# A two-layer RWKV-7 / convolution backbone: the block merge of each triangular inverse split from its solve, with buffers of its own time

## The chip, the cores and the metric

The kernel runs on one core of a Trainium2 chip. The metric is the device time of one execution in microseconds (us); shorter is better. The engines are called PE (TensorE, matrix products), DVE (VectorE), ACT (ScalarE), POOL (GpSimd) and SP (SyncE, which issues transfers).

## The reference, cut to what matters

Layer 0 mixes tokens by a bidirectional RWKV-7 recurrence over 16 heads of 64 channels, next to a gated short convolution. A context of 256 tokens runs first and hands its final states to the latent sequence of 512 tokens. Layer 1 is a Conformer convolution module. The change lies in layer 0's recurrence:

```python
def wkv_scan(S0, r, decay, k, v, kk, a, reverse):
    def step(S, inp):
        r_t, w_t, k_t, v_t, kk_t, a_t = inp
        sa = jnp.einsum("bhvk,bhk->bhv", S, -kk_t)
        S = (S * w_t[:, :, None, :]
             + sa[..., None] * (kk_t * a_t)[:, :, None, :]
             + v_t[..., None] * k_t[:, :, None, :])
        return S, jnp.einsum("bhvk,bhk->bhv", S, r_t)
    ...
yac, S_f, S_b = rwkv_seq(rwkv_prep(hc, ...), zero, zero, r_k, lnx_w, lnx_b, ctx_out)
ya, _, _ = rwkv_seq(rwkv_prep(h, ...), S_f, S_b, r_k, lnx_w, lnx_b, True)
yb = bg * dwconv(cg * xb, sc_w, seg_len)
y = jnp.concatenate([ya * jax.nn.silu(za), yb * jax.nn.silu(zb)], axis=-1) @ w_out
```

## The kernel before, in words

**Tiling.** The recurrence is computed in chunks of 64 tokens. Inside a chunk it is a triangular system, whose 64x64 inverse is formed for each head, direction and chunk; from chunk to chunk only a state is handed on. The work is cut into 12 "states": four of the context (c0 to c3, four heads and four chunks each) and eight of the latent sequence (l0 to l7, two heads and eight chunks each). Both directions and all heads of a state lie side by side, so that 32 inverses are formed at once.

**One state passes through these steps.**
- *Preparation*: projections of r, k, v (`prep_ctx`, `prep_lat`), then `light`, which runs `lightz` for each direction: decays and gates into the tiles P, a and kd (each of these tags has one buffer), and from them the factors AR and BK.
- *heavy*: the products `pal` on PE, masked by DVE into E (L601), the transposed BK (`pbl`, copied by ACT at L612), the diagonal 32x32 blocks of E copied by ACT into the tile Nt (L618), v transposed (`pvl`, L629) and the bonus (`pbonl`, L636).
- *solve*: DVE transposes Nt into X (L650) and inverts all 32x32 diagonal blocks by 31 elimination steps of two operations each (L656, L658); the result is Y.
- *merge* (inside `solve`, L659 to L681): two inverted 32x32 blocks become the inverse of a 64x64 block. DVE transposes Y into R1 (L661) and R1 into R2 (L662), ACT copies R1 into E (L667), PE multiplies 64 blocks (called M1 below), ACT copies the product to Gs (L676), PE multiplies 64 blocks again (M2), and ACT copies that into E (L681). R1 is the tile Nt, R2 is Y's tile and Gs a half of X's tile.
- *chain*: over the chunks in turn, PE's products into `zo` and `uh`, ACT's copies of them to O (Ol, L756) and UV (L762), and DVE's update of the state H (L769). A chain step reads E, and its products are pinned to the written order.

There is one Nt for all states, and E, UV and BKt of the latent states exist twice.

**Order.** The main loop runs chain(s) and then, by the letters of `STAGE`, the work of the states after it: P prepares s+2, L and H are `light` and `heavy` of s+2, S is `solve` of s+1, O the bonus of s+1, F the fills and the output of s, C the gated convolution. A scheduler takes the letters' order as priorities and merges these streams into one order for each engine, so PE fills the chain's waits with wide products: `pcg`, `pxb`, `pbg` and `pzb` of the convolution branch, and in the context `plr`, `plk` and others. Each wide product runs three times, since weights are split into a high and a low half (`wh`, `wl`, L126 on ACT and L127 on DVE). All matrix products go through the helper on L57.

Of the kernel before, what the change touches and what calls it, by code (L numbers as in the profile page):

```python
# [15 lines left out]
P = 128  # L16
# [15 lines left out]
CONV_AFTER = (0, 2, 7, 6)  # L32
PA_ORDER = ((0, 1), (1, 0), (1, 1), (0, 0))
HEAVY = ("VBOAN", "ANBV")
STAGE = ("OFPLSH", "OSPLHFC")
FILL_R = (0, 0, 2, 3, 4, 4, 4, 4)
FILL_Z = (0, 1, 1, 1, 3, 3, 3, 3)
ZR = (slice(0, 64), slice(64, 128))
# [13 lines left out]
def kernel(ctx: ExitStack, tc: tile.TileContext, I: dict, out: bass.AP):  # L52
# [3 lines left out]
    def mm(o, lhsT, rhs, start, stop):  # L56
        return T.matmul(o, lhsT, rhs, start=start, stop=stop)  # L57
# [36 lines left out]
    def col(nm, j, n=1):  # L94
        gi, off, _ = colpos[nm]
        return colt[gi][:, off + j : off + j + n]
# [80 lines left out]
    def w(tag, name, dt=F32):  # L177
        return wk.tile([P, SIZE.get(tag, 512)], dt, tag=tag, name=name, bufs=NBUF.get(tag, 1))

    def ch3(t, x=CH):  # L180
        return t.rearrange("p (c x) -> p c x", x=x)

    def small(name, shape):
        return cvp.tile(shape, F32, tag=name, name=name)
# [11 lines left out]
    Nt = small("Nt", [P, 16, 32])  # L196
# [196 lines left out]
    def prep_ctx(b, between=None):  # L393
        st = state(False, b)
        for which in (1, 2):
            st["rkv"[which]] = t = w("rkv"[which] + "_", "rkv"[which] + st["nm"])
            for p, cs in st["parts"]:
                project(p, which, t[:, cs])
                if between:
                    between()  # L400
        return st
# [240 lines left out]
    def solve(st):  # L642
        nm, E = st["nm"], st["E"]
        Xt = w("X", "X" + nm)
        X = Xt.rearrange("p (a b) -> p a b", b=32)
        Yt = w("Y", "Y" + nm)
        Y = Yt.rearrange("p (a b) -> p a b", b=16)
        tmp = w("xtmp", "xtmp" + nm)
        nc.gpsimd.dma_start(Y, I["unit"])
        V.transpose(X.rearrange("p (r s) t -> p t r s", r=2),  # L650
                    Nt.rearrange("p q t -> p t q").unsqueeze(2).to_broadcast([P, 32, 2, 16]))
        for i in range(31, 0, -1):
            c0 = i // 2
            m = 16 - c0
            tv = tmp[:, : i * m].rearrange("p (a b) -> p a b", b=m)
            V.tensor_tensor(out=tv, in0=X[:, :i, i : i + 1].to_broadcast([P, i, m]),  # L656
                            in1=Y[:, i : i + 1, c0:].to_broadcast([P, i, m]), op=ALU.mult)
            V.tensor_tensor(out=Y[:, :i, c0:], in0=Y[:, :i, c0:], in1=tv, op=ALU.add)  # L658
        R1 = Nt  # L659
        R2 = Yt.rearrange("p (a b) -> p a b", b=32)  # L660
        V.transpose(R1.rearrange("p q (c r) -> p c r q", r=2), Y.rearrange("p (a b) c -> p c a b", a=2))  # L661
        V.transpose(R2, R1)  # L662
        Gs = Xt[:, 0:512].rearrange("p (a b) -> p a b", b=32)
        for z in range(2):
            for b in range(2):
                rs = slice(64 * z + 32 * b, 64 * z + 32 * b + 32)
                S.copy(E[rs, 1 - z, :, 32 * b : 32 * b + 32], R1[rs])  # L667
        pg = px = uhs[1]
        top = [slice(64 * z, 64 * z + 32) for z in range(2)]
        low = [slice(64 * z + 32, 64 * z + 64) for z in range(2)]  # L670
        for q in range(16):
            for z in range(2):
                mm(pg[low[z], q * 32 : q * 32 + 32], E[top[z], 1 - z, q, 32:64], R2[top[z], q, :],
                   True, True)
        for z in range(2):
            S.copy(Gs[low[z]], ch3(pg[low[z]], 32))  # L676
        for q in range(16):
            for z in range(2):
                mm(px[top[z], q * 32 : q * 32 + 32], Gs[low[z], q, :], R1[low[z], q, :], True, True)
        for z in range(2):  # L680
            S.copy(E[top[z], 1 - z, :, 32:64], ch3(px[top[z]], 32))  # L681
# [179 lines left out]
    def rest(n=1):  # L861
        for g in range(mv["n"], min(mv["n"] + n, 16)):
            half_, kt = g // 8, g % 8
            if kt == 0:
                mv["acc"] = uhs[0] if half_ == 0 else ps.tile([P, 512], F32, tag="zo", name="mpb", bufs=2)
                V.memset(mv["acc"], 0.0)
            for q in range(4):
                u = 4 * half_ + q
                layer, c0 = (0, 2 * D + 512 * u) if u < 2 else (1, 512 * (u - 2))
                if g < 2:  # L870
                    with tc.issue_after(env["last"].ins):
                        nc.sync.dma_start(mws[q], I["mod_w"][layer, kt * P : (kt + 1) * P, c0 : c0 + 512])
                    continue
                nc.gpsimd.dma_start(mws[q], I["mod_w"][layer, kt * P : (kt + 1) * P, c0 : c0 + 512])
            for q in range(4):
                mm(mv["acc"][32 * q : 32 * q + 2, :], s2[:, kt, :], mws[q], kt == 0, kt == KT - 1)
            if kt == KT - 1:
                rested(half_, mv["acc"])
        mv["n"] += n

    def rested(half_, acc):
        row = w("HP", f"mrow{half_}")
        mt = ps_at(f"mr{half_}")
        for b in range(2):
            S.copy(row, acc[:, 256 * b : 256 * b + 256])
            for j in range(2):
                T.transpose(mt[:, (2 * b + j) * P : (2 * b + j + 1) * P], row[:, j * P : (j + 1) * P], ident)
        src = mt.rearrange("p (j q x) -> p q j x", j=4, q=4)[:, :, :, 0]
        for dst, u0, n, bias in (((gate0, 0, 2, col("mod_b0", 16, 8)), (modc1[:, 0:8], 2, 2, col("mod_b1", 0, 8)))
                                 if half_ == 0 else ((modc1[:, 8:24], 0, 4, col("mod_b1", 8, 16)),)):  # L890
            V.tensor_tensor(out=dst.rearrange("p (q j) -> p q j", q=n), in0=src[:, u0 : u0 + n],
                            in1=bias.rearrange("p (q j) -> p q j", q=n), op=ALU.add)
        if half_ == 0:
            V.memset(acc, 0.0)
# [9 lines left out]
    sts = [prep_ctx(0, rest)]  # L904
# [3 lines left out]
    heavy(sts[0])  # L908
    rest()
    solve(sts[0])  # L910
    rest(2)
    sts.append(prep_ctx(1, rest))
    light(sts[1])
# [2 lines left out]
    for s in range(12):  # L916
        st = sts[s]
        if s < 4:
            for i in range(NCTX):
                chain_ctx(st, i)  # L920
        else:
            for i in range(NLAT):
                chain_lat(st, i)
        if s == 11:
            finish(st)
            break
        for x in STAGE[s >= 4]:
            if x == "S":
                solve(sts[s + 1])
            elif x == "O":  # L930
                if sts[s + 1]["lat"]:
                    sts[s + 1]["po"]()
            elif x == "P" and s < 10:
                sts.append(prep_ctx(s + 2) if s < 2 else prep_lat(s - 2))
            elif x == "L" and s < 10:
                light(sts[s + 2], st)
            elif x == "H" and s < 10:
                heavy(sts[s + 2], st)
            elif x == "F":
                fills(s + 1)  # L940
                if s >= 4:
                    finish(st)
            elif x == "C":
                conv_branch(s - 3, st["anchor"])
                if s == 10:
                    rs.close()
                    op = rs.enter_context(tc.tile_pool(name="op", bufs=1, reuse_waits="tile", side="right"))
                    env["lo"] = V
        if s == 3:
            G.memset(cx[:, :, 0:66:65], 0.0)  # L950
            conv_branch(0)
            V.scalar_tensor_tensor(out=gsc1, in0=modc1[:, 8:16], scalar=1.0, in1=col("g_pre1", 0, 8),
                                   op0=ALU.add, op1=ALU.mult)
            gv = ss6
            V.tensor_tensor(out=gv[:, 0:8], in0=gate0, in1=col("g_post", 0, 8), op=ALU.mult)
            V.tensor_tensor(out=gv[:, 8:16], in0=modc1[:, 16:24], in1=col("g_post", 8, 8), op=ALU.mult)
            pgv = ps_at("pgv")
            T.transpose(pgv[:16, :P], gv, ident)
            gvr = w("xtmp", "gvr")[0:16, 0:P]
            S.copy(gvr, pgv[:16, :P])  # L960
            nc.sync.dma_start(gvd.rearrange("a (k p) -> (a k) p", p=P), gvr)
# [26 lines left out]
    with ExitStack() as l1:  # L988
# [118 lines left out]
        for n in range(4):  # L1107
            ws = {}
            for part, tag in ((1, "wa"), (0, "wb")):
                for kt in range(0, KT, 2):  # L1110
# [3 lines left out]
                    w = split(src, f"wc{n}{part}{kt}", tag)  # L1114
# [3 lines left out]
            for m in range(4):  # L1118
# [10 lines left out]
                a = lt("a", f"a{n}{m}")  # L1129
# [20 lines left out]
        for j in range(16):  # L1150
# [5 lines left out]
            t = t2[:, j % 2 * 512 : j % 2 * 512 + 512]  # L1156
# [4 lines left out]
        for j in range(16):  # L1161
# [10 lines left out]
            t = lt("wb" if j < 10 else "xr", f"y{j}", F32R)  # L1172
# [12 lines left out]
        for n in range(2):  # L1185
# [17 lines left out]
            for m in range(4):  # L1203
# [3 lines left out]
                t = lt("a", f"sq{m}{n}") if n else None  # L1207
# [93 lines left out]
```

## Time and profile before

| | |
|---|---|
| time, three runs | 1476.52, 1486.42, 1487.33 us; median 1486.42 |
| profiled execution | time 1487.99 us, span 1486.2 us, so 1.8 us outside the span |
| PE, DVE, ACT busy | 1421.5, 955.8, 777.6 us of the span |
| mean granted TensorE clock | 0.976 of full |
| PE's clock over 40 slices of 37 us | 0.9 or more but for the slices from 223 us (0.7), 446 us (0.6) and 1077 us (0.8) |

A time line starts at the span's start. Layer 0's context states run until about 520 us, its latent states until about 990, and the rest is the output projection and layer 1. In the rows below, a line names the code line, the engine, the operation and its tiles, out<-in, with buffer numbers left out; `[1.77 <-ACT Nt L618]` is idle time in front of the instruction and what ended it.

### The profile page before, as it was taken

How to read it: one execution, taken by the hardware profiler on the slowest of the kernel's cores; microseconds unless marked ns; L12 is line 12 of the kernel's file. 1: busy time of each engine (PE TensorE's matmuls, PEld its weight loads, DVE VectorE, ACT ScalarE, POOL GpSimd, SP SyncE). 2: the span in 40 equal slices, each digit the busy share in tenths (PEclk: the TensorE clock that was granted, in tenths of full speed). 3: DMA queues.
4: the chain of work that ended last, by engine and by line, in shares of the span. 5: the costliest groups of instructions: out<-in, count | busy, mean ns of one | idle time of the engine just before them, and what ended most of it. 6: DMA issues, size and time to landing. Idle time of an engine off the chain costs nothing.

```text
span 1486.2 us, 29753 instructions
## 1 busy us (share of the span) xinstructions
PE 1421.5 (96%) x11921; PEld 1015.5 (68%) x11921; DVE 955.8 (64%) x2250; ACT 777.6 (52%) x1564; POOL 128.5 (9%) x250
## 2 busy tenths in 40 slices
PE   6899999999999999999999999999889999999998
PEld 1464667878767666666666666677767777688876
DVE  2665576668696978888788787657545535544333
ACT  4536364374755575755757556546544313463222
POOL 2022210000110101011010100011100000000000
PEclk9999997999996999999999999999989999999999
DMA  8754431312232312231222213358603203133322
GB/s 324 216 168 161 154 110 58 103 58 75 74 104 65 90 60 79 62 94 45 86 73 59 90 30 100 131 201 304 208 30 114 86 28 113 46 97 99 98 87 85
DMA packets 137627, 158.55 MB, mean 107 GB/s; under 512 B 15375, under 2 KB 104143, under 8 KB 137369
## 3 DMA queue, kind: packets, MB, share of 16 engines
q1 hardware_dynamic: 121104, 106.47, 23.0%
q0 software_dynamic: 15312, 48.99, 10.3%
q8 instruction: 94, 1.54, 0.4%
q10 hardware_dynamic: 1072, 1.19, 0.2%
q14 instruction: 45, 0.37, 0.1%
HBM read 138.33 MB, written 18.28 MB: 105 GB/s over the span
## 4 chain that ended last, share of the span: by engine, by line
PE 47%; ACT 7%; DVE 5%; issue 1%; DMA 1%; DVEq 0%; SPq 0%; ACTq 0%
PE pu L57 12%; PE f L57 6%; PE pz L57 6%; PE o L57 4%; PE zol L57 3%; PE pbg L57 3%; PE pxb L57 3%; PE uh L57 2%; PE pal L57 1%; PE pc L57 1%; PE px L57 1%; PE pcg L57 1%; ACT Nt L618 1%; DVE E L601 1%; ACT UV L629 1%
## 5 line engine op out<-in xcount | busy, mean ns | idle before, releaser
L57 PE MATMUL o<-wh,y 128*128 128x512 f32 x248 | 80.2, 401 | 1.0 <-ACT wh L126 1.0
L57 PE MATMUL pal<-ARl,BKl 64*128 64x128 f32 x512 | 59.1, 311 | 6.9 <-DVE xtmpc L656 4.3
L658 DVE TENSOR_TENSOR Yl<-Yl,xtmpl 128x126 f32<-128x126 f32 (+22 forms) x248 | 61.9, 250 | 2.2
L656 DVE TENSOR_TENSOR xtmpl<-Xl,Yl 128x126 f32<-128x126 f32 (+22 forms) x248 | 61.9, 249 | 2.0
L57 PEld LDWEIGHTS pal<-ARl,BKl 64*128 64x128 f32 x512 | 44.2, 199 | 26.4 <-DVE E L601 6.1
L1136 ACT CAST ah<-a 64x512 fp32r<-64x512 f32 x32 | 19.8, 618 | 72.9 <-DVE a L1131 72.5
L57 PE MATMUL zol<-UV,E 64*64 64x64 f32 (+1 forms) x1024 | 54.2, 221 | 0.0
L57 PEld LDWEIGHTS o<-wh,y 128*128 128x128 f32 x248 | 46.7, 191 | 10.9 <-ACT wh L126 1.1
L57 PE MATMUL o<-wl,y 128*128 128x512 f32 x124 | 50.3, 405 | 3.9 <-DVE wl L127 3.9
L57 PE MATMUL zol<-Hl,ARl 64*64 64x64 f32 x896 | 50.2, 230 | 1.9 <-DVE Hl L769 1.9
L762 ACT COPY UV<-uh 64x128 f32<-64x128 f32 x128 | 33.4, 261 | 33.4 <-PE uh L57 31.1
L601 DVE TENSOR_TENSOR E<-pal,maskE 128x512 f32<-128x512 f32 x64 | 43.4, 683 | 11.0 <-PE pal L57 10.9
L127 DVE TENSOR_TENSOR wl<-wr,wh 128x1024 fp32r<-128x1024 f32 x28 | 37.0, 1320 | 20.9 <-ACT wh L126 20.7
L57 PEld LDWEIGHTS zol<-Hl,ARl 64*64 64x64 f32 x896 | 35.1, 133 | 20.7 <-issue 16.8
L769 DVE SCALAR_TENSOR_TENSOR Hl<-uh,PCl,HPl 128x64 f32<-128x64 f32 x112 | 26.6, 279 | 30.6 <-PE uh L57 22.6
L57 PEld LDWEIGHTS uh<-UV,BKt 128*64 128x64 f32 x704 | 26.8, 138 | 28.0 <-ACT UV L762 21.6
L57 PEld LDWEIGHTS zol<-UV,E 64*64 64x64 f32 (+1 forms) x1024 | 42.4, 136 | 2.8 <-ACT UV L762 2.1
L1131 DVE TENSOR_TENSOR a<-pu,a 128x512 f32<-128x512 f32 x16 | 11.0, 689 | 51.3 <-PE pu L57 49.0
L1092 DVE SCALAR_TENSOR_TENSOR pr<-px,dbe,What 119x512 f32<-119x512 f32 x32 | 22.5, 746 | 32.8 <-PE px L57 32.7
L126 ACT CAST whcg<-wrcg 128x512 fp32r<-128x512 f32 x16 | 9.9, 619 | 64.0 <-DMA wrcg<-in_ev_w_in_dram 60.1
L126 ACT CAST wh<-wr 128x1024 fp32r<-128x1024 f32 x28 | 29.4, 1049 | 23.5 <-PE o L57 11.0
L57 PE MATMUL uh<-UV,BKt 128*64 128x64 f32 x704 | 37.0, 234 | 4.0 <-ACT UV L762 2.5
(935 smaller groups left out, 4306.5 us busy)
## 6 DMA issues: line engine op xcount, KB each, us to landing
wr<-in_ev_w_out_dram SPq DMA_DIRECT2D x28, 512.0 KB, 5.4
mwo<-in_mod_w_dram POOLq DMA_DIRECT2D x28, 256.0 KB, 3.3
mwr<-in_mod_w_dram POOLq DMA_DIRECT2D x28, 256.0 KB, 4.2
ectx<-in_mod_w_dram SPq DMA_DIRECT2D x12, 512.0 KB, 5.1
wrk<-in_ev_w_in_dram SPq DMA_DIRECT2D x16, 256.0 KB, 2.8
wrv<-in_ev_w_in_dram SPq DMA_DIRECT2D x16, 256.0 KB, 3.7
wrr<-in_ev_w_in_dram SPq DMA_DIRECT2D x16, 256.0 KB, 2.9
wrza<-in_ev_w_in_dram SPq DMA_DIRECT2D x16, 256.0 KB, 2.8
```

What stands on the lines that cost most here:

```text
L57: return T.matmul(o, lhsT, rhs, start=start, stop=stop)
L126: S.copy(hi, raw)
L127: env["lo"].tensor_tensor(out=lo, in0=raw, in1=hi, op=ALU.subtract)
L601: V.tensor_tensor(out=E[:, h, z * NLAT + c0 : z * NLAT + c0 + m, :], in0=pas[h], in1=maskE[:, z * (1 + h) : z * (1 + h) + 1, 0:x].to_broad ...
L618: S.copy(Nt[rs], E[rs, h, :, 32 * b : 32 * b + 32])
L629: S.copy(dst, src if lat or not z else src[:, :, ::-1, :])
L656: V.tensor_tensor(out=tv, in0=X[:, :i, i : i + 1].to_broadcast([P, i, m]), in1=Y[:, i : i + 1, c0:].to_broadcast([P, i, m]), op=ALU.mult)
L658: V.tensor_tensor(out=Y[:, :i, c0:], in0=Y[:, :i, c0:], in1=tv, op=ALU.add)
L762: u_ = S.copy(UV[ZR[1 - h], i : 2 * nch - i : 2 * nch - 1 - 2 * i, ZR[h]], uh[ZR[1 - h], 0:2, :])
L769: h_ = V.scalar_tensor_tensor(out=Hn[:, z, :], in0=uh[:, 2 + z, :], scalar=PC[z][:, i : i + 1], in1=HP[:, z, :], op0=ALU.mult, op1=ALU.add)
L1092: V.scalar_tensor_tensor(out=pr[s][:NPROD], in0=px[s][:NPROD], scalar=dbe[:, 0:1], in1=What[:, n * 512 : n * 512 + 512], op0=ALU.add, op1= ...
L1136: S.copy(ahl[s][hr], a[hr])
```

## The change

The merge becomes a function of its own. R1, R2 and Gs get tiles of the tags kd, a and P, which `lightz` uses as well and which have one buffer each, so a merge waits until the `light` before it has read them, and the next `light` waits for the merge. Nt is no longer written by a merge, nor are Y's and X's tiles. In `STAGE` the letter M stands behind L: the merge of s+1 is issued behind the light phase of s+2. Before, it was issued inside S.

```diff
-STAGE = ("OFPLSH", "OSPLHFC")
+STAGE = ("OFPLSMH", "OSPLMHFC")
@@ solve
-        R1 = Nt
-        R2 = Yt.rearrange("p (a b) -> p a b", b=32)
+        st["Y"] = Y
+
+    def merge(st):
+        nm, E, Y = st["nm"], st["E"], st["Y"]
+        R1, R2, Gs = (w(t, f"{t}m{nm}")[:, 0:512].rearrange("p (a b) -> p a b", b=32) for t in ("kd", "a", "P"))
         V.transpose(R1.rearrange("p q (c r) -> p c r q", r=2), Y.rearrange("p (a b) c -> p c a b", a=2))
         V.transpose(R2, R1)
-        Gs = Xt[:, 0:512].rearrange("p (a b) -> p a b", b=32)
         for z in range(2):
@@ main loop
     solve(sts[0])
+    merge(sts[0])
     rest(2)
@@
             if x == "S":
                 solve(sts[s + 1])
+            elif x == "M":
+                merge(sts[s + 1])
```

On DVE, before the change, these rows begin with the merge of l4 (L661, L662); the X transposes of l5 are L650, its elimination L656 and L658, and L769 the first update of chain l4.

```order
L661 STREAM_TRANSPOSE Nt_112<-Yl4_8087 128x32x16
L662 STREAM_TRANSPOSE Yl4_8087<-Nt_112 128x512
L811 SCALAR_TENSOR_TENSOR bonl3_6613<-po3_8456,hcol_76,bonl3_6613 128x512
L812 SCALAR_TENSOR_TENSOR bonl3_6613<-bonl3_6613,hcol_76,gz3_8473 128x512
L636 SCALAR_TENSOR_TENSOR bonl5_8267<-pbonl5_8910,vl5_8230 128x512
L650 STREAM_TRANSPOSE Xl5_8913<-Nt_112 128x32x32
L477 STREAM_TRANSPOSE rncl6_9076<-ssl6_9074 128x512
L790 SCALAR_TENSOR_TENSOR gzb4_8634<-gzb4_8634,pzb4_8609 128x512
L656 TENSOR_TENSOR xtmpl5_8915<-Xl5_8913,Yl5_8914 128x31
```

After the change, the merge of l4 (now L664 and L665) stands 29 rows ahead of the X transposes of l5. These are the rows from the last masks of l5 on; between them and the first update of chain l4 follow 32 more.

```order
L601 TENSOR_TENSOR E110_5060<-pal5001_8391,maskE_108 128x512
L601 TENSOR_TENSOR E110_5060<-pal5000_8390,maskE_108 128x512
L813 SCALAR_TENSOR_TENSOR bonl3_6557<-po3_8483,hcol_76,bonl3_6557 128x512
L814 SCALAR_TENSOR_TENSOR bonl3_6557<-bonl3_6557,hcol_76,gz3_8500 128x512
L650 STREAM_TRANSPOSE Xl5_8940<-Nt_112 128x32x32
L656 TENSOR_TENSOR xtmpl5_8942<-Xl5_8940,Yl5_8941 128x31
L658 TENSOR_TENSOR Yl5_8941<-Yl5_8941,xtmpl5_8942 128x31
L656 TENSOR_TENSOR xtmpl5_8942<-Xl5_8940,Yl5_8941 128x30
```

So the masks of the next state moved behind the merge, and the next elimination now runs in a block ahead of the chain's first update: 27 of its operations, where two stood there before.

On PE, before, M1 of l4 is the first row with 32x32, M2 the last; `zol4_0` is the start of chain l4.

```order
L57 MATMUL po3_8456<-ident_60,Ol3_7815 64x64 x7
L57 MATMUL uh1_124<-Yl4_8087,E100_4343 32x32 x32
L57 MATMUL pzb4_8609<-hll_119,whzb41_8604 128x512
L57 MATMUL zol4_0_8643<-h0_4_7400,ARl41_7493 64x64 x2
L57 MATMUL zol4_0_8643<-UV100_4342,E100_4343 64x64 x4
L57 MATMUL uh1_124<-Nt_112,Xl4_8086 32x32 x32
```

After, M1 of l4 stands among the `pal` products of l5's heavy phase, each row of which is a pair.

```order
L57 MATMUL pbg4_8598<-hll_119,whbg40_8587 128x512
L57 MATMUL uh1_124<-aml4_8278,E100_4355 32x32 x32
L57 MATMUL pal5111_8379<-ARl51_8270,BKl51_8271 128x128
L57 MATMUL pbg4_8598<-hlh_118,wlbg40_8588 128x512
L57 MATMUL pbg4_8598<-hlh_118,whbg40_8587 128x512
L57 MATMUL pal5110_8378<-ARl51_8270,BKl51_8271 128x128
```

There M2 follows after four more `pal` rows, and chain l4 begins 93 rows behind M1: `pbg`, `pal`, `po`, `pbl`, `pvl` and all 24 `pzb` stand between, most of which stood ahead of M1 before.

On ACT, before, the merge of l5 is L667, L676 and L681, and the Nt copies of l6 are L618.

```order
L667 COPY E110_5045<-Nt_112 32x16x32 x4
L676 COPY Xl5_8913<-uh1_124 32x512 x2
L618 COPY Nt_112<-E100_4343 32x512 x2
L629 COPY UV100_4342<-pvl6_9246 64x8x64 x2
L681 COPY E110_5045<-uh1_124 32x16x32 x2
L618 COPY Nt_112<-E100_4343 32x512 x2
```

After, they are L669, L678 and L683, and the four Nt copies stand together behind all of them.

```order
L669 COPY E110_5060<-kdml5_9107 32x16x32 x4
L678 COPY Pml5_9109<-uh1_124 32x512 x2
L126 CAST whzb50_9455<-wrzb50_9454 128x512
L839 ACTIVATE yb5_9412<-cx_111,hcol_76 128x512
L473 ACTIVATE sql7_9855<-kl7_9838,cols1_67 128x512
L683 COPY E110_5060<-uh1_124 32x16x32 x2
L446 CAST lwhl7_9850<-lwrl7_9845 128x512
L126 CAST whzb51_9461<-wrzb51_9460 128x512
L618 COPY Nt_112<-E100_4355 32x512 x4
```

Of each engine the instructions are the same in kind and number; only their places differ.

## Rows read from the trace of the kernel before

**Rows 1.** Page, part 1: busy time, share of the span, instructions.
```profile
PE 1421.5 (96%) x11921; PEld 1015.5 (68%) x11921; DVE 955.8 (64%) x2250; ACT 777.6 (52%) x1564; POOL 128.5 (9%) x250
```
**Rows 2.** Windows between merges: length; busy us of PE, PEld, DVE, ACT, POOL; clock.
```profile
711.40:773.20 61.80, 59.08 (x781) 40.06 (x777) 51.14 (x153) 39.92 (x94) 6.71 (x12) 1.00 0.25 71
...
sum 416.80, PE 399.85 PEld 272.37 DVE 341.19 ACT 269.29 POOL 38.98; mean PE 57.12 PEld 38.91 DVE 48.74 ACT 38.47 POOL 5.57
```
**Rows 3.** Waits of PE, 711.4 to 773.2: total us, times, longest.
```profile
PE uh L57 <- ACT Ol L756: 0.9, 1, 0.9
PE pzb L57 <- DVE wlzb L127: 0.5, 1, 0.5
PE uh L57 <- ACT UV L762: 0.4, 1, 0.4
PE pal L57 <- DVE E L601: 0.3, 1, 0.3
PE zol L57 <- DVE Hl L769: 0.2, 1, 0.2
```
**Rows 4.** Timeline of DVE around the merge of l3: start us, duration us.
```profile
711.40 1.10 DVE L661 STREAM_TRANSPOSE Nt<-Yl 128x512 f32<-128x512 f32 x1
712.54 0.71 DVE L662 STREAM_TRANSPOSE Yl<-Nt 128x512 f32<-128x512 f32 x1
713.17 0.71 DVE L811 SCALAR_TENSOR_TENSOR bonl<-po,hcol,bonl 128x512 f32<-128x512 f32 x1
...
718.70 0.69 DVE L636 SCALAR_TENSOR_TENSOR bonl<-pbonl,vl 128x512 f32<-128x512 f32 x1 [4.03 <-PE pbonl L57]
721.16 2.01 DVE L650 STREAM_TRANSPOSE Xl<-Nt 128x1024 f32<-128x1024 f32 x1 [1.77 <-ACT Nt L618]
```
**Rows 5.** Timeline of ACT at the same place.
```profile
712.53 2.52 ACT L667 COPY E<-Nt 32x512 f32<-32x512 f32 x4 [1.13 <-DVE Nt L661]
715.07 1.17 ACT L676 COPY Xl<-uh 32x512 f32<-32x512 f32 x2
716.27 1.24 ACT L618 COPY Nt<-E 32x512 f32<-32x512 f32 x2
...
719.88 1.24 ACT L618 COPY Nt<-E 32x512 f32<-32x512 f32 x2
```
**Rows 6.** Timeline of DVE: elimination operations side by side, and interleaved.
```profile
421.19 0.30 DVE L656 TENSOR_TENSOR xtmpc<-Xc,Yc 128x136 f32<-128x136 f32 x1
421.52 0.30 DVE L658 TENSOR_TENSOR Yc<-Yc,xtmpc 128x136 f32<-128x136 f32 x1
...
727.24 0.22 DVE L656 TENSOR_TENSOR xtmpl<-Xl,Yl 128x58 f32<-128x58 f32 x1
...
727.49 0.22 DVE L658 TENSOR_TENSOR Yl<-Yl,xtmpl 128x58 f32<-128x58 f32 x1
```
**Rows 7.** Timeline of PE from the end of chain l2 to the start of chain l3.
```profile
691.90 0.71 PE L57 MATMUL zol<-UV,E 128*64 128x64 f32 x8
...
692.88 0.40 PE L57 MATMUL pbg<-hll,whbg 128*128 128x512 f32 x1
693.11 0.40 PE L57 MATMUL pbg<-hlh,wlbg 128*128 128x512 f32 x1
...
696.59 1.16 PE L57 MATMUL pal<-ARl,BKl 64*128 64x128 f32 x14
...
713.30 1.20 PE L57 MATMUL uh<-Yl,E 32*32 32x32 f32 x64
...
715.80 0.45 PE L57 MATMUL zol<-h,ARl 64*64 64x64 f32 x8
```
**Rows 8.** Two waits of PE in the context, and the half-clock window behind the first.
```profile
PE plr L57 <- ACT whr L126: 1.2, 1, 1.2
```
```profile
PE pbc L576 <- ACT BKt L612: 1.1, 2, 0.9
```
```profile
217.50:238.00 20.50, 20.50 (x103) 15.33 (x102) 5.42 (x8) 5.79 (x11) 0.85 (x2) 0.50 0.26 78
```

## The prediction, made before the change was timed

> **What bounds the kernel now.** I read the busy times first: TensorE (PE) is busy for 96% of the span, VectorE (DVE) for 64% [rows 1]. So only the rest of PE's time can be won, and only where PE waits. The windows come next, cut at the merges of the latent states (one merge to the next is a "stage"). A stage lasts 61.80 us, with PE busy for 59.08 and DVE for 51.14, at the full clock, and over the seven stages from 523.7 to 940.5 us PE is busy for 399.85 of 416.80 us [rows 2]. All PE idleness in the part that the change reorders most is therefore 416.80 - 399.85 = 16.95 us, 1.1% of the time. Third, the waits of PE in one stage: 0.9 us of the first chain step on ScalarE's (ACT's) Ol copy, 0.5 on wlzb, 0.4 on UV, 0.3 on E, 0.2 on Hl, together 2.3 of the 2.7 [rows 3]. The largest stands where the merge stands.
>
> What the merge does there is read from the lists of DVE and ACT. L661 and L662 run at 711.40 and 712.54; then DVE idles for 4.03 us and, in front of the solve's X transposes (L650), for 1.77 us, behind ACT's Nt copies [rows 4]. ACT does the merge's copies first (2.52 and 1.17 us), and the Nt copies (L618) stand at 716.27 and 719.88, behind and between them [rows 5]. That is the wait that the change takes away. It is a wait of DVE, which has 10.7 us to spare in the stage; PE feels it only as far as ACT's queue delays Ol.
>
> **The change, part by part.**
> The merge does the same two transposes, eight copies and 128 small products, so its work costs nothing new: no instruction is added on PE, DVE or ACT, and no DMA. Only places and buffers move.
>
> *Nt freed.* R1 no longer overwrites Nt, so the four Nt copies go together and don't wait for L667 to read R1. The first chain step now has the 24 pzb products and pbl, pvl, po between the merge and itself, and Ol's copy stands behind no merge copy: the 0.95 us go. M1 also no longer stands right behind the last po; I give its remaining 0.3 us to that (the rest of 2.7 less 2.3 is spread in shorter gaps). Removed: 1.25 us a stage, at six merges (l1 to l6), at most 7.5 us. The other 1.4 us a stage (wlzb, UV, E, Hl) have causes that the change doesn't touch, and stay.
>
> *M2 closer to M1.* Before, five pzb and sixteen chain products stood between the two halves; the chain's first came 1.3 us after M1's end (714.50 to 715.80 [rows 7]) and M2 behind it, which hid the Gs copies of 1.17 us [rows 5]. After, one pal, two pbg and five pal rows stand there. Priced by 14 pal in 1.16 us and a step of 0.23 us for a 512-wide product [rows 7], that is 12 x 0.083 + 2 x 0.23 = 1.5 us. The copy takes 1.17 and has to be signalled both ways; the nearest case of that is M1, which starts 713.30 - 712.53 = 0.8 us after its first copy began although each copy is 0.63 (2.52 / 4) [rows 5, 7]. 1.17 + 2 x 0.17 = 1.5, so nothing at best, and if another ACT copy of 0.6 stands ahead, 0.6. I take 0.3.
>
> *Elimination ahead of the chain.* This speaks against the change. In its order of DVE, from the merge of l4 (L664) to the first update that the chain needs (Hl4_0) stand 65 rows, before only 14. Among them are X and 27 elimination operations of l5; there were two. I add them up: 23 operations of 512 columns at the spacing of 0.63 (712.54 to 713.17 [rows 4]) 14.5, L664 1.1, X 2.0, 27 eliminations of 0.28 (between the 0.33 and 0.22 below) 7.6, two half-size ones 0.8, thirteen tiny ones of 0.13 (about half of the 0.25 below) 1.7: 27.7 us. X must also wait for the Nt copies that follow the last mask, 2.5 us (4 x 0.62 [rows 5]) of which L813 and L814 cover 1.2: 1.3, in all 29.0. On PE, M1 starts 1.9 us after L661 [rows 4, 7]. From the end of the last chain product (691.90 + 0.71) to the chain's start at 715.80 are 23.2 us [rows 7], of them 1.1 waits (0.3, 0.5 and the 0.3 at M1): 22.1. After, behind M1's start, five pbg (1.2) and 32 pal (2.7) of these are already done, and M2 (1.2, as M1 takes 1.20) comes in: 19.4. From the chain's start to the first product that reads Hl stand 40 small products, pbonl, ssl and five pcg, about 5 us. Sum 1.9 + 19.4 + 5 = 26.3, and with the waits of E, wlzb and M2 (0.3 + 0.5 + 0.3) 27.4. So DVE comes 29.0 - 27.4 = 1.6 us late. I take 1.5 us for l4 to l6, and 0.3 for l1 to l3, where fewer eliminations (7 to 19 adjacent, against 20 to 27) lie ahead of the chain. The bounds: nothing below, where the DVE queue is done in time; above, DVE's whole idle time in front of the bonus, 4.0 [rows 4], if none of it is filled by what now runs early.
>
> An adjacent elimination operation depends on the one before. In the profile 421.19 to 421.52 is 0.33 us for an operation of 0.30, while 727.24 to 727.49 holds one of 0.22 and a tiny one beside it in 0.25 [rows 6]: alone it costs about 0.03 more than its length, interleaved about 0.09 less. With some 16 more of them side by side that is 16 x 0.12 = 1.9 us of DVE time a stage, 51.1 to 53 of 61.8, still not DVE-bound; in the sum above it is the 0.28.
> [...]
>
> *pal bank.* The masks (L601) of the next heavy now come behind the merge on DVE; where L664 and L665 (1.81 us) stand ahead of one, PE waits for a bank. A quarter of it, 0.4, at l4 to l6; nothing to 1.8.
>
> *Context.* The merge of c1 moves behind the light phase of c2. Just there PE waits 1.1 us for BKt in front of pbc now [rows 8], and M1 (1.2 us) comes to stand among these products, so that it can fill that wait: -1.1, and nothing if the copies of the merge delay BKt by as much. At 216.8 PE waits 1.2 for whr, and then runs at the clock of 1.2 GHz from 217.5 to 238.0 [rows 8]; the full clock would do that in half, so the stretch costs 10.25. In the new order whr is cast a slot earlier. Whether that stretch goes can't be derived; I leave it in the sum. The merges of c3 and l0 hardly move.
>
> **Sum.** l1 to l3: -1.25 + 0.3 + 0.3 = -0.65, three times -1.95. l4 to l6: -1.25 + 0.3 + 1.5 + 0.4 = +0.95, three times +2.85. Latent states: +0.9. Context -1.1. Together -0.2. The profiled execution's span is 1486.2 us and its time 1487.99, 1.6 above the median of the three runs; 1487.99 - 0.2 = 1487.8 against its own time, and 1486.42 - 0.2 = 1486.2 against the median. I predict 1486.
>
> **Rivals.**
> *Faster: all of PE's stage gaps close.* If the DVE queue is done before the chain needs Hl (sum under 27.4), the 16.95 us can go, and with the whr stretch 10.25 more. For it: the same gap repeats in every stage, and Nt's reuse is the only tie between two states on DVE. Against: more than half of the gap hangs on wlzb, UV, E and Hl [rows 3]. Time: 1486.4 - 17 - 1.1 = 1468, with the clock 1458; half the gaps and the clock, 1467. Chance 0.22.
> A rule of the Trainium skill stands beside this rival (Perfetto Trace Analysis, "Optimization Strategy"): a gap that repeats on the engine that should be saturated can mean too few buffers for the next tile. Here the trace shows such a gap, but mostly with other releasers.
>
> *Slower: DVE decides the chain's start.* Place: the first chain steps of l1 to l6, behind X and the eliminations. Price: the upper bound of 4.0 us a stage, less 1.25 removed, plus 0.7 for M2 and masks, +3.45 at six stages = 20.7: 1486.4 + 20.7 - 1.1 = 1506. For it: 65 rows against 14, and my two sums differ by 1.6 us of 29. Against: DVE has 10.7 us a stage to spare, and whatever is done early is not done later. It decides the sign at a wait of 0.55 a stage (1.25 - 0.7), and gives over 1% at 3.2. Chance 0.18.
>
> *Slower clock at c1.* M1, M2 and pbc of c1 now stand close together among few wide products; a new half-speed stretch like the one from 217.5 (20.5 us long) would cost up to 10 us: 1496. Nothing in a row says that it must come. Chance 0.12.
>
> *The move reaches nothing.* Nt's copies wait for the masks (L601), not for the merge, and the stage keeps its 61.8 us: 1486. Speaks for it that L618 can only follow the last mask. It lies inside my forecast's own range.
>
> **How the numbers follow.** My forecast, with the move that reaches nothing, has 0.48 and its own range is 1478 to 1494 (the bounds above, half of them, and one clock stretch either way). What a measurement of this kernel can tell from no change is about 1%, 14.9 us: below 1471.5 faster, above 1501.3 slower. The faster rival has 0.22, nearly all of it below that bound; of the slower one 0.17 lies above, of the clock 0.01. So faster 0.21, same 0.61, slower 0.18. The range leaves out the outer tenth on either side: 1467 to 1502.
>
> **What would show each step.** Right: in a stage of the profile after, PE's wait on Ol is gone, DVE waits less in front of L650, and a wait on Hl of 1 to 2 us appears at the first chain step of l4 to l6, with PE's busy time of a stage as before, 59.1. The stage from merge to merge keeps 61 to 63 us. The stretch from 217.5 at the lower clock is there. Wrong: stages of 60 us or less (the faster rival), or an Hl wait of 3 us and stages over 64 (the slower one), or a clock below full behind c1's merge.

## The result, and the profile after

The changed kernel takes 1474.31 us (median of 16 runs, 1466.83 to 1481.93), the kernel before 1485.76 us (16 runs beside them, 1475.26 to 1494.88). The ratio is 0.9928, with a 95% interval of 0.9907 to 0.9949. The change makes the kernel 11 us faster, which is within the 1% that I called "same", but clear of noise. I predicted 1486.

The page of the changed kernel, part 1 (busy us, share, instructions), answers [rows 1]; its span is 1471.2 us.

```profile
PE 1414.4 (96%) x11921; PEld 1013.6 (69%) x11921; DVE 961.5 (65%) x2250; ACT 777.1 (53%) x1564; POOL 129.0 (9%) x250
```

The merges now stand at another place in a stage, so I cut both traces at the starts of the latent chains. These are the windows from chain l3 to chain l4, of the kernel before and then of the changed one (length; busy us and instructions of PE, PEld, DVE, ACT, POOL; clock).

```profile
715.80:777.60 61.80, 59.07 (x774) 40.05 (x773) 51.14 (x153) 39.91 (x94) 6.72 (x13) 1.00 0.25 71
```
```profile
708.20:768.00 59.80, 59.62 (x775) 40.64 (x774) 53.57 (x156) 40.24 (x94) 6.73 (x12) 1.00 0.25 73
```

PE does the same work, and 2.73 us of idle time have become 0.18. DVE is busy for 2.4 us longer. From the start of chain l0 to that of chain l7, PE's waits by what released them were these before (total us, times, longest):

```profile
PE uh L57 <- ACT Ol L756: 4.9, 6, 1.0
PE pzb L57 <- DVE wlzb L127: 3.2, 6, 0.6
PE uh L57 <- ACT UV L762: 2.5, 6, 0.6
PE zol L57 <- DVE Hl L769: 1.9, 6, 0.5
PE pal L57 <- DVE E L601: 1.4, 5, 0.3
PE uh L57 <- DVE Yl L662: 0.7, 3, 0.3
PE pbl L576 <- ACT BKt L612: 0.5, 1, 0.5
```

and these after (the lines behind the merge have moved by 2 to 5):

```profile
PE uh L57 <- ACT UV L764: 2.7, 7, 0.9
PE pal L57 <- DVE E L601: 2.3, 3, 1.5
PE pbl L576 <- ACT BKt L612: 1.3, 3, 0.6
PE uh L57 <- DVE aml L665: 0.8, 1, 0.8
PE zol L57 <- DVE Hl L771: 0.7, 3, 0.3
PE uh L57 <- ACT Ol L758: 0.6, 2, 0.4
PE uh L57 <- ACT Pml L678: 0.5, 1, 0.5
```

Ol falls from 4.9 to 0.6, as expected; wlzb from 3.2 to less than the last row, and Hl from 1.9 to 0.7, neither of which I had expected. Of E's 2.3 us, 1.8 lie in the first stage, from l0 to l1.

**How runs are compared below.** The times of one kernel differ by up to 22 us, and a run that took longer mostly had a lower mean clock. In each run the product of span and mean granted clock is about the time that the same work would take at 2.4 GHz throughout; span less that product is what the stretches at 1.2 GHz cost. It is an estimate, but its mean is steadier than the time (standard error 0.3 to 1.1 us). It is too low by half of the time for which PE waits within such stretches, since a wait doesn't run faster at the full clock: PE idles there for 20 us in e5's profiled run, and for 5 to 8 us in each of the others, so that this matters in e5 alone. "PE idle" is PE's idle time from chain l0's start to chain l7's, in the profiled run.

| kernel | median us | ratio, 95% interval | at full clock | lost to the clock | PE idle, latent |
|---|---|---|---|---|---|
| before | 1485.3 to 1486.5 | 1 | 1452.3 to 1453.1 | 30 to 34 | 17.1 |
| the change | 1474.3 | 0.9928 (0.9907, 0.9949) | 1440.9 | 31 | 9.4 |
| e2, context only | 1485.5 | 0.9994 (0.9962, 1.0026) | 1451.4 | 32 | 17.0 |
| e3, latent only | 1475.9 | 0.9929 (0.9894, 0.9965) | 1442.0 | 32 | 9.1 |
| e4, R1 only | 1482.0 | 0.9957 (0.9919, 0.9994) | 1441.5 | 40 | 8.8 |
| e10, R1 only, latent only | 1475.8 | 0.9925 (0.9894, 0.9957) | 1442.9 | 31 | 8.9 |
| e6, R2 and Gs only | 1486.8 | 1.0026 (0.9994, 1.0058) | 1448.4 | 38 | 15.6 |
| e5, tiles without the later place | 1540.0 | 1.0366 (1.0326, 1.0406) | 1454.0 | 86 | 43.5 |
| e8, change + 2 us of DVE a stage | 1479.5 | 0.9936 (0.9910, 0.9962) | 1442.8 | 33 | 12.0 |
| e9, before + 2 us of DVE a stage | 1498.0 | 1.0063 (1.0034, 1.0092) | 1460.0 | 36 | 23.7 |
| e12, before - 14 DVE operations a stage | 1484.1 | 0.9993 (0.9966, 1.0021) | 1436.4 | 47 | 8.4 |
| e13, change - 14 DVE operations a stage | 1473.8 | 0.9915 (0.9882, 0.9947) | 1441.8 | 30 | 9.5 |
| e11, merge a letter later | 1471.2 | 0.9893 (0.9856, 0.9930) | 1437.4 | 32 | 7.4 |

### The profile page after: what moved, and what is told of

The parts are those of the page before. It is cut to its first block, busy times and chain, and to the rows that moved or that the text cites. A ratio compares the mean times of both kernels' runs of the same rounds, so it can differ in the third digit from the quotient of the medians.

```text
span 1471.2 us, 29740 instructions
## 1 busy us (share of the span) xinstructions
PE 1414.4 (96%) x11921; PEld 1013.6 (69%) x11921; DVE 961.5 (65%) x2250; ACT 777.1 (53%) x1564; POOL 129.0 (9%) x250
## 3 DMA queue, kind: packets, MB, share of 16 engines
q0 software_dynamic: 15312, 48.99, 10.2%
## 5 line engine op out<-in xcount | busy, mean ns | idle before, releaser
L656 DVE TENSOR_TENSOR xtmpl<-Xl,Yl 128x126 f32<-128x126 f32 (+22 forms) x248 | 62.0, 250 | 4.6 <-DMA Yl<-in_unit_dram 1.5
L658 DVE TENSOR_TENSOR Yl<-Yl,xtmpl 128x126 f32<-128x126 f32 (+22 forms) x248 | 62.4, 251 | 3.6
L127 DVE TENSOR_TENSOR wl<-wr,wh 128x1024 fp32r<-128x1024 f32 x28 | 36.8, 1314 | 22.5 <-ACT wh L126 22.3
L57 PEld LDWEIGHTS zol<-Hl,ARl 64*64 64x64 f32 x896 | 34.9, 133 | 20.5 <-issue 13.3
L771 DVE SCALAR_TENSOR_TENSOR Hl<-uh,PCl,HPl 128x64 f32<-128x64 f32 x112 | 26.5, 278 | 27.4 <-PE uh L57 20.7
L57 PEld LDWEIGHTS uh<-Ol,E 64*64 64x64 f32 x512 | 19.9, 133 | 23.7 <-ACT Ol L758 14.2
```

The source lines that it names most:

```text
L127: env["lo"].tensor_tensor(out=lo, in0=raw, in1=hi, op=ALU.subtract)
L771: h_ = V.scalar_tensor_tensor(out=Hn[:, z, :], in0=uh[:, 2 + z, :], scalar=PC[z][:, i : i + 1], in1=HP[:, z, :], op0=ALU.mult, op1=ALU.add)
```

## The experiments

**The letter alone does nothing.** With R1, R2 and Gs back in Nt, Y's and X's tiles, the changed kernel has the kernel before's order of instructions on every engine: the tie of the tiles, not the letter, had put the merge where it was.

**Where the gain lies: e2 and e3.** In both the tiles depend on the state:

```diff
-        R1, R2, Gs = (w(t, f"{t}m{nm}")[:, 0:512].rearrange("p (a b) -> p a b", b=32) for t in ("kd", "a", "P"))
+        if not st["lat"]:                  # e2; in e3: if st["lat"]
+            R1, R2, Gs = (w(t, f"{t}m{nm}")[:, 0:512].rearrange("p (a b) -> p a b", b=32) for t in ("kd", "a", "P"))
+        else:
+            R1 = Nt
+            R2 = st["Yt"].rearrange("p (a b) -> p a b", b=32)
+            Gs = st["Xt"][:, 0:512].rearrange("p (a b) -> p a b", b=32)
-STAGE = ("OFPLSMH", "OSPLMHFC")
+STAGE = ("OFPLSMH", "OSMPLHFC")            # e2 alone
```

> The four context states use the new tiles (kd, a, P) for their merges; the eight latent states merge as before, inside the solve, in Nt, Y and X. Theory A (the gain has two parts: about 10 us from the stretch at 1.2 GHz that began at 217.5 us and is gone after the change, and about 5 us net from the latent stages): ratio 0.993 to 0.996, no half-clock stretch between 210 and 240 us, latent stages of 61.8 us as before. Rival B (half-clock stretches fall by chance, and all of the gain is in the latent stages): ratio 0.999 to 1.001.

> The reverse: only the latent states use the new tiles, with their merge behind the next light phase; the context states merge in Nt, Y and X as before. Theory A: ratio 0.996 to 0.998 (about -5 us), latent stages of 60 us, the half-clock stretch at 217.5 us there as before. Rival B: ratio 0.991 to 0.994, the whole gain.

e2 gives a ratio of 0.9994, e3 one of 0.9929. As far as these runs can tell, the whole gain is in the latent states. The profiled runs agree: from chain l0 to chain l7, both at the full clock, the kernel before and then e3 take

```profile
530.50:950.40 419.90, 402.79 (x5326) 274.69 (x5322) 342.76 (x1029) 268.16 (x631) 38.98 (x70) 1.00 0.23 67
```
```profile
530.40:940.10 409.70, 400.65 (x5317) 276.16 (x5315) 349.87 (x1029) 267.28 (x631) 38.94 (x70) 1.00 0.23 69
```

which is 10.2 us less, 8.1 of it idle time of PE. Theory A is wrong, though I had read it from two profiles: the profiled run of the change reaches chain l0 10.4 us earlier than that of the kernel before (520.1 against 530.5 us), since the stretch at 217.5 [rows 8] is missing. That was the luck of one run. In its context, e3 has the same order of instructions as the kernel before, up to the merge of l0. These are the windows 210 to 240 and 300 to 340 of the kernel before and of e3 (clock in the third column from the end):

```profile
210.00:240.00 30.00, 28.60 (x172) 20.71 (x171) 13.73 (x20) 14.81 (x30) 1.62 (x3) 0.66 0.24 72
300.00:340.00 40.00, 37.48 (x499) 28.95 (x497) 27.26 (x62) 29.79 (x65) 1.62 (x3) 1.00 0.20 60
```
```profile
210.00:240.00 30.00, 28.62 (x257) 20.70 (x256) 19.36 (x37) 18.13 (x38) 2.16 (x4) 0.94 0.33 100
300.00:340.00 40.00, 38.50 (x406) 31.93 (x406) 21.40 (x46) 23.20 (x52) 0.54 (x1) 0.74 0.12 34
```

The same order of instructions ran slowly behind 217 us in one execution and behind 314 us in the other. Such a stretch can't be put down to a change by two profiles.

**Which tile counts: e4, e10 and e6.**

```diff
-        R1, R2, Gs = (w(t, f"{t}m{nm}")[:, 0:512].rearrange("p (a b) -> p a b", b=32) for t in ("kd", "a", "P"))
+        R1 = w("kd", f"kdm{nm}")[:, 0:512].rearrange("p (a b) -> p a b", b=32)   # e10: Nt in the context
+        R2 = st["Yt"].rearrange("p (a b) -> p a b", b=32)
+        Gs = st["Xt"][:, 0:512].rearrange("p (a b) -> p a b", b=32)
```

e6 is the complement of e4: R1 is Nt, and R2 and Gs are the new tiles of a and P.

> In all states R1 alone moves, from Nt to the tile kd; R2 stays in Y's tile and Gs in X's, and the merge is issued behind the next light phase. Theory C (a free Nt is what counts, as the diff's words and my prediction have it): stages of 60 us and the ratio of the whole change, 0.991 to 0.995. Rival D (Nt alone frees little, because the next X transposes then wait for M2 to read Gs in X's tile): ratio 0.997 to 1.001, stages of 61 to 62 us, DVE's wait in front of the X transposes still there and put down to PE.

> The complement: R1 stays in Nt, R2 and Gs move to the tiles a and P, and the merge is issued behind the next light phase. Theory C: Nt still ties the next state's Nt copies to the merge, stages of 61.8 us, ratio 0.998 to 1.002. Rival D: part of the gain, 0.994 to 0.997. If e4 and e6 both give nothing, the gain needs all three tiles to be free.

> R1 alone moves from Nt to kd, and in the latent states alone; the context and R2, Gs are as before. Theory C (in the latent states the free Nt is the whole gain): ratio 0.991 to 0.995, span times granted clock (the time the work would take at the full clock) 10 to 11 us below the kernel before, as when all three tiles moved. Rival D (R2 and Gs are needed too): 0.995 to 0.999, 4 to 7 us below.

e10 has the ratio of the whole change (0.9925) and, within the errors, the full-clock time of e3 (1442.9 against 1442.0), with R1 in kd and no other tile moved. It lies 9.4 us below the kernel before, near the 10 to 11 of theory C and above the 7 of rival D. So theory C holds for the latent states: Nt is what has to be free. e6 has nothing to show in time. At the full clock it is 4 us below the kernel before, and it loses 5 us more to the clock. e4's ratio, 0.9957, lies between the forecasts of C and D. It differs from e10 in the context alone; it has nearly the same full-clock time and loses 8 us more to the clock. Whether R1's place in the context causes these stretches is open, as e2, with all three tiles there, has none in excess.

**Is the later place needed: e5 and e11.**

```diff
-STAGE = ("OFPLSMH", "OSPLMHFC")
+STAGE = ("OFPLSMH", "OSMPLHFC")   # e5
+STAGE = ("OFPLSMH", "OSPLHMFC")   # e11
```

> The new tiles in all states, but the latent merge issued right behind the elimination, ahead of the next preparation, as before (the letter M stands behind S). Now the next light phase has to wait for the merge before it may write kd, a and P. Theory E (the later place is needed, because otherwise the preparation of the next state waits): ratio 1.002 to 1.02, with waits of PE on AR or BK or on masks in the latent stages. Rival F (the free Nt is all that counts): ratio 0.991 to 0.995.

> The changed kernel with the latent merge issued one letter later, behind the heavy phase of the next state (OSPLHMFC). In the order of the engines the merge still stands where the elimination ends, right behind the chain before. If the free Nt is what counts, 0.991 to 0.995, as the change. If the exact place of the merge among the next masks counts, more than 3 us off it in either direction.

e5 is slower by 3.7%, and this row of PE's waits from 525 to 985 us names the cause that theory E expects, a preparation that comes late:

```profile
PE pal L57 <- ACT BKl L557: 27.2, 8, 5.4
```

I had put its size at 2% at most. PE's idle time rises by 26 us, and the granted clock over the latent states falls to 0.88; together they make the 54 us, and as the waits lie within the slow stretches, the two columns of the table don't part them. So the three tiles of the preparation pay only together with the later place. What a second buffer for Nt, without these tiles, would give was not run.

e11 is at least as good as the change. Its interval, 0.9856 to 0.9930, overlaps with the change's, so whether it is better, by 3 us in the medians, is not settled. It beats the kernel before.

**Which engine is late: e8, e9, e12 and e13.** After the result I had two theories for the unexpected part. The prediction's own slower rival says that DVE is now at the edge; theory I says that DVE was at the edge before, and is now less so. e8 and e9 add DVE work to both kernels; e12 and e13 take some away by leaving out every fourth elimination step, so that their inverses are incomplete.

```diff
         V.transpose(X.rearrange("p (r s) t -> p t r s", r=2),
                     Nt.rearrange("p q t -> p t q").unsqueeze(2).to_broadcast([P, 32, 2, 16]))
+        if st["lat"]:                      # e8 on the change, e9 on the kernel before
+            V.transpose(X.rearrange("p (r s) t -> p t r s", r=2),
+                        Nt.rearrange("p q t -> p t q").unsqueeze(2).to_broadcast([P, 32, 2, 16]))
@@
         for i in range(31, 0, -1):
+            if st["lat"] and i % 4 == 0:  # e12 on the kernel before, e13 on the change
+                continue
```

> The changed kernel, with the X transposes of each latent solve done twice, which only adds about 2.0 us of DVE work in front of the elimination. Theory G (in the changed kernel DVE's queue between a merge and the chain's first update is as long as PE's work, 28.0 against 28.5 us, so it is at the edge): PE waits on Hl or on the merge in the latent stages, 1 to 2 us a stage, ratio to the kernel before 0.998 to 1.004 (8 to 16 us more than the change alone). Rival H (DVE has enough to spare in a stage): 0.991 to 0.995, as without the second transposes.

> The kernel before with the same second X transposes. Theory G: DVE idles for 5.8 us just there before the change, so 2.0 us more cost at most a third of what they cost in the changed kernel: ratio 1.000 to 1.004. Rival H: 1.000. If it costs 8 us or more (1.006 and up), the DVE queue was as tight before as after, and the change did not tighten it.

> The kernel before with every fourth elimination step of the latent solves left out (7 of 31 steps, 14 DVE operations, about 3.5 us of DVE work a stage; the inverses are then incomplete). Theory I (before the change DVE is behind in the second half of a stage, because it stands idle for 5.8 us at the merge, and PE's waits on wlzb, E and Hl come from that): these waits close, 5 to 9 us less, ratio 0.994 to 0.997. Rival J (these waits come from where ACT's and PE's work stands, not from DVE's load): at most 2 us less, 0.999 to 1.001.

> The changed kernel with the same 14 operations of each latent solve left out. Theory I: DVE is no longer behind, so there is little to win: 0 to 3 us less than the changed kernel, ratio to the kernel before 0.990 to 0.993. Rival J: the same difference as between the kernel before with and without them; if it wins more here than there (5 us and more), DVE is the tighter engine after the change, as the prediction's slower rival has it.

Theory G fell in e8, whose ratio of 0.9936 (0.9910 to 0.9962) lies below its 0.998 to 1.004, and narrowly in e9, whose interval begins at 1.0034. At the full clock the second X transposes cost 1.9 us in the changed kernel (1442.8 against 1440.9) and 7.7 us in the kernel before (1460.0 against 1452.3); by the median times it is 5.2 and 11.7. The kernel before, which by its windows had 10.7 us of DVE to spare, was the one that could less well take 2 us more. In e9's waits of PE, DVE's elimination appears as a releaser that the kernel before didn't have:

```profile
PE uh L57 <- ACT UV L765: 6.2, 14, 1.2
PE uh L57 <- ACT Ol L759: 3.7, 9, 0.8
PE zol L57 <- DVE xtmpl L659: 3.6, 7, 0.7
```

Taking DVE work away points the same way at the full clock: e12 is 16.7 us below the kernel before (1436.4 against 1453.1), and its waits on wlzb and Hl are gone from the list, though E's rose from 1.4 to 2.5 us; e13 is where the changed kernel is (1441.8 against 1440.9). But by the time e12's ratio, 0.9993, is what rival J forecast, and theory I's forecast of 0.994 to 0.997 failed: by the table the stretches at 1.2 GHz cost 16 us more there and hide the whole gain. Why they do is open. The profiled runs show 9.8 us less idle time of PE in e12 (its span less its busy time is 54.9 us, against 64.7), so part of the 16.7 is not seen there.

Nor do the four kernels differ by the same DVE work alone, since the scheduler orders each of them anew. The eight added transposes take 16.1 us, but DVE's busy time in the whole execution rose by 10.0 us in e8 and by 18.1 in e9; the omission lowered it by 10.9 in e12 and by 16.0 in e13. And e12's order has hardly any of the kernel before's idle time in front of X: from chain l0 to chain l7 DVE waits there and for pbonl for 5.1 us, against 34.5. So theory I is the better supported of the two, but these four runs don't show it by themselves.

## Why the prediction was right or wrong

The range (1467 to 1502) and the likeliest class held, because the range is 35 us wide and the gain below 1%; the mechanism behind the point held in part only, and that the time still fell inside the range owes more to its width. The point was 12 us too high, and the sum's +0.9 us for the latent states had the wrong sign: e3 shows 10.3 us less at the full clock (1442.0 against 1452.3). The stage of 59.80 us is under the 60 that I had named as a sign of the faster rival, and the Hl wait of 1 to 2 us did not come.

**Removed, Ol and M1: Ol near in size.** I took 7.5 us at most for six stages, 5.7 of it for Ol, which went down by 4.3. M1's wait (on Yl before, on aml after) is 0.7 us before and 0.8 after, all of the latter in the first stage, so the 1.8 us that I took for it were not there.

**"The other 1.4 us a stage have causes that the change doesn't touch, and stay": this step failed.** wlzb gave up to 3.2 us, and Hl gave 1.2, where I had expected its wait to grow. I took a wait's releaser for its cause. These are the rows of the kernel before around the wait on wlzb at 704.49; first ACT, then DVE.

```profile
694.70 0.62 ACT L126 CAST whzb<-wrzb 128x512 fp32r<-128x512 f32 x1 [0.23 <-PE pbg L57]
```
```profile
703.52 0.24 DVE L656 TENSOR_TENSOR xtmpl<-Xl,Yl 128x91 f32<-128x91 f32 x1
703.68 0.16 DVE L425 SCALAR_TENSOR_TENSOR orq<-orq 128x8 f32<-128x8 f32 x1
703.75 0.68 DVE L127 TENSOR_TENSOR wlzb<-wrzb,whzb 128x512 fp32r<-128x512 f32 x1
```

DVE's input whzb was ready at 695.3; L127 started 8.4 us later, in a DVE queue whose only wait from 695.5 on was one of 0.53 us, between elimination operations that were due before the merge. DVE was behind. What had put it behind, by my reading, are the 4.03 and 1.77 us ahead of X [rows 4]: I had called them time "to spare", while nothing but X and what follows it stood in that queue. Of the 10.7 us, 5.8 were locked up there, and what was left was too little where it was wanted. The first of the two ended with pbonl on PE, not with Nt, but it stands in the same order of DVE. From chain l0 to chain l7 they were these before:

```profile
DVE bonl L636 <- PE pbonl L57: 22.9, 7, 4.0
DVE Xl L650 <- ACT Nt L618: 11.6, 7, 3.2
```

and these in e10, where R1 alone had left Nt, and where PE's waits on wlzb and Hl are gone too:

```profile
DVE Xl L650 <- ACT Nt L618: 6.4, 3, 3.6
DVE Xl L650 <- PE uh L57: 3.1, 1, 3.1
DVE bonl L636 <- PE pbonl L57: 2.5, 1, 2.5
```

In e6, where R1 stayed, this is left, and PE waits for DVE elsewhere, 5.3 us on E and 3.5 on aml:

```profile
DVE Xl L650 <- ACT Nt L618: 18.6, 5, 5.4
```

So e10 and e6 show that the tie by Nt causes the waits in front of X; the wait for pbonl fell in e6 too, to 3.1 us, and hangs on the order. That these waits of DVE are what makes PE wait later in the stage is argued from the rows and from e8 and e9, not shown. After the change, the waits of DVE from chain l3 to chain l4 have neither; the two stages behind it have neither as well, the two ahead of it still 1.5 and 1.4 us in front of X:

```profile
DVE Hl L771 <- PE uh L57: 2.7, 4, 1.0
DVE Ol L784 <- PE zol L57: 1.4, 1, 1.4
DVE bonl L813 <- PE po L57: 0.5, 1, 0.5
```

This is the prediction's faster rival in mechanism, to which I gave 0.22: the tie by Nt between two states on DVE. Its price of 17 us was too high, since 9.4 us of idle time stay. The Trainium skill's rule on repeated gaps and too few buffers, which stood beside it (Perfetto Trace Analysis, "Optimization Strategy"), agrees with e10, where moving one tile, R1, out of Nt removes half of PE's idle time in the latent states (17.1 to 8.9 us). I had set it aside because the gap had "other releasers"; of these, wlzb and Hl went with the tie.

**Elimination ahead of the chain: both sums were off.** DVE and PE around the merge and the first step of chain l4, after:

```profile
744.77 1.14 DVE L664 STREAM_TRANSPOSE kdml<-Yl 128x512 f32<-128x512 f32 x1
...
758.66 2.06 DVE L650 STREAM_TRANSPOSE Xl<-Nt 128x1024 f32<-128x1024 f32 x1
...
772.77 0.43 DVE L771 SCALAR_TENSOR_TENSOR Hl<-uh,PCl,HPl 128x64 f32<-128x64 f32 x2
```
```profile
747.44 1.20 PE L57 MATMUL uh<-aml,E 32*32 32x32 f32 x64
...
767.98 0.45 PE L57 MATMUL zol<-h,ARl 64*64 64x64 f32 x8
...
773.26 0.45 PE L57 MATMUL zol<-Hl,ARl 64*64 64x64 f32 x8
```

From the merge to Hl are 28.0 us on DVE, for which I had 29.0. On PE the first product that reads Hl starts 28.5 us after the merge; I had 27.4, with M1 0.8 us too early, the work up to the chain 1.1 us and its first products 0.3 us short, and 1.1 us of waits too many. Two sums of 28 us, each a few per cent off, can't tell a wait of 1.5 us from none. The wait on Hl is 0.3 us at most. I booked 5.4 us for it at six stages, the largest term against the change, and in e8, with a second X transpose in each solve, it is 1.5 us in four waits: DVE's queue is long there, but full of work that isn't due at once. The price of side-by-side elimination came out near (DVE busy 53.57 us a stage, I had 53), and it doesn't bind.

**M2 and the pal bank.** I took 1.8 and 1.2 us; M2's wait is 0.5, and E's rose by 0.9; in the first stage it is 1.8, in the others less than before.

**Context.** I took -1.1 us. e2 shows 1452.3 - 1451.4 = 0.9 us less at the full clock, with a standard error of 0.7, which can't be told from nothing, and the reason I gave is not what the rows show. The wait on BKt is gone from the changed kernel, and at the same place these two came, which fit no step of mine:

```profile
PE pck L57 <- ACT whk L126: 1.4, 1, 1.4
PE uh L57 <- DVE amc L665: 1.4, 1, 1.4
```

**The clock.** Leaving the stretch from 217.5 us in the sum was right on average (30 to 34 us lost before, 31 after), though the profiles alone say otherwise. The rival of a slower clock at c1 has its sign in the changed kernel's profiled run, 6.8 us at 1.2 GHz from 307.6 us, just where c1 is merged; but a longer stretch stands near there in e3 too (20.5 us from 314.1), whose context is that of the kernel before, and the mean loss didn't grow.

## What to carry to other kernels

An engine's idle time is to spare only if other work can be done in it: idle time in front of an instruction with the queue behind it can be as lost as busy time, and one should subtract it before saying how much an engine has left. A wait's releaser is the place where lateness shows; before one says that a change doesn't touch it, one asks whether the releaser started late, and behind what. And a gain of 1% is to be read from many runs, here with time and clock taken apart, and not from where two profiles differ.

## What the runs showed of the hardware

Stretches of PE at 1.2 GHz cost the kernel before 30 to 34 us a run on average, and they move by themselves: with the same order of the context, 20.5 us from 217.5 us in one execution and 20.5 from 314.1 in another. With DVE work left out of the kernel before, this loss is 47 us instead of 30 (e12); with the same work left out of the changed kernel it stays at 30 (e13). In e5, where PE waits for the preparation in every stage, its clock over the latent states is 0.88, in the kernel before 1.00. On DVE, the eight second X transposes of 2.0 us each raised the busy time by 10.0 us in one order of its queue (e8) and by 18.1 in another (e9).
